# Attention weights times values as two rounded products on the full array, with the weights split by ScalarE and VectorE

## The chip, the cores and the metric

The kernel runs on one core of one Trainium2 chip. The metric is the device time of one execution in microseconds. The engines are TensorE (PE, whose weight loads the profile lists apart as PEld), VectorE (DVE), ScalarE (ACT), GpSimd (POOL) and SyncE (SP, which issues the DMAs).

## What is computed

One inference step of a one-layer trunk on 1024 prompt tokens and 8 running streams of 16 new tokens: three token mixers side by side (stick-breaking attention, Mamba-2, forgetting attention "FoX"), then cross-attention into 256 memory tokens, then a SwiGLU feed-forward, all in float32. The change touches the two attention mixers for the prompt, four heads of 64 columns each:

```
def sb_attend(q, k, v, q_pos, k_pos):
    z = einsum('bqhd,bkhd->bhqk', q, k) * (HEAD_DIM ** -0.5)
    valid = k_pos[None, :] < q_pos[:, None]
    log_keep = where(valid, log_sigmoid(-z), 0.0)
    after = cumsum(log_keep, axis=3, reverse=True) - log_keep
    w = where(valid, exp(log_sigmoid(z) + after), 0.0)
    return einsum('bhqk,bkhd->bqhd', w, v)

def fox_attend(q, k, v, fq, fk, q_pos, k_pos):
    s = einsum('bqhd,bkhd->bhqk', q, k) * (HEAD_DIM ** -0.5) + (fq - fk)
    p = softmax(where(k_pos[None, :] <= q_pos[:, None], s, -inf))
    return einsum('bhqk,bkhd->bqhd', p, v)
```

The last line of each, weights times values, is the product that changes.

## The kernel before

Almost every large product of the kernel is made of three products of rounded numbers: each float32 operand is split into a high part (the value rounded to the short type `fp32r`) and a low part (the rest, rounded too), and `mm3` (L327 to L330) adds high x high, high x low and low x high in PSUM. Such a product goes through PE as one record per instruction.

The prompt's weights times values are not done so. For one head and one pair of 128-query blocks (`qp` = 0 to 3, so 256 queries), `prompt_av` (L571) walks over the key blocks in pairs `kp`. `weights_T` (L575) transposes the weights of two key blocks and two query blocks on PE (L580, into a PSUM bank of the pool `pst`, three banks), and ACT copies the bank to SBUF in float32 (L583, a tile of the pool `pt`, four tiles). The products (L595) take the values `vt` of 128 keys, 64 columns, as the stationary operand and the copied weights as the moving one, both plain float32. For `qp` over 0 the results of even and odd key blocks go to PSUM partitions 0 to 63 and 64 to 127, that is, to the two column halves of PE's array, and four products of two `kp` are issued together, alternating between the halves, so that the two halves can work side by side. For `qp` 0 both go to the first half. At the end ACT copies the upper half and DVE adds the lower (L603, L604; for `qp` 0 one copy, L606), and a DMA writes the 64 x 256 result.

Before that, `load_stacks` (L501) loads for each of the eight heads (four of each mixer) the stacked queries and keys (six DMAs, L507 and L508) and the values (one DMA, L510), from scratch memory in DRAM. `sb_rows` (L513) and `fox_rows` (L528) compute the weights: products on PE (L562 to L565), sigmoids or exponentials on ACT (L519, L520, L542), a scan or a reduction on DVE (L522, L536), and for the first mixer a multiplication on POOL (L132).

The order of the work is set by the scheduler of the tile framework, which places every instruction by its own estimate of time, with hints: `together` (L332) asks that its instructions stand one behind the other, and `hp("av")` (L359) gives `prompt_av` a higher priority. The attention units run woven with other work: the projections of the input (L328 to L330, evacuated at L452 to L456 and L488), the same two attentions of the running streams (L874, L889, L934), the convolution (L772) and the Mamba-2 steps (L1070 to L1162). Each engine then runs its own list strictly in the order given.

Of the kernel before, what the change touches and what calls it, by code (L numbers as in the profile page):

```python
# [8 lines left out]
F32 = mybir.dt.float32  # L9
# [3 lines left out]
ALU = mybir.AluOpType  # L13
# [4 lines left out]
P = 128  # L18
D = 1024
KT = D // P  # L20
SEQ = 1024
# [36 lines left out]
def f32(x):  # L58
    return x.bitcast(F32)
# [3 lines left out]
def tile_hybrid_step(ctx: ExitStack, tc: tile.TileContext, a: dict):  # L63
# [28 lines left out]
    def st_t(dt=F32R):  # L92
        return stp.tile([P, 1024], dt, tag="st", name="st")
# [10 lines left out]
    def pt_t(dt=F32R):  # L104
        return ptp.tile([P, 512], dt, tag="pt", name="pt")
# [129 lines left out]
    v_sc = [dram([T, 256], F32, f"vsc{i}") for i in range(2)]  # L235
# [96 lines left out]
    def together(emits):  # L332

        with tc.high_priority(GROUP):
            first = emits[0]()
            with tc.issue_after(first.ins):
                for f in emits[1:]:
                    f()
# [162 lines left out]
    def load_stacks(m, h):  # L501

        nb, r0 = h // 2, (h % 2) * 64
        iq, ik = 4 * m + nb, 4 * m + 2 + nb
        qs, kh, kl = st_t(), st_t(), st_t()
        for t, i, x0, x1 in ((qs, iq, 0, 1), (kh, ik, 0, 0), (kl, ik, 1, 1)):
            SP.dma_start(out=f32(t[0:64, :]), in_=f32(qk_sc[i, x0, r0:r0 + 64, 0:SEQ]))  # L507
            SP.dma_start(out=f32(t[64:128, :]), in_=f32(qk_sc[i, x1, r0:r0 + 64, 0:SEQ]))  # L508
        vt = st_t(F32)[:, :512].rearrange("p (k d) -> p k d", d=64)
        SP.dma_start(out=vt, in_=v_sc[m][0:SEQ, h * 64:(h + 1) * 64].rearrange("(k p) d -> p k d", p=P))  # L510
        return qs, kh, kl, vt

    def sb_rows(n, pieces):  # L513

# [56 lines left out]
    def prompt_av(h, qp, w0, w1, vt, kt_row):  # L571

        nk = 2 * qp + 2
        po = pO()
        def weights_T(kp):  # L575
            tp = pT()
            o = 0
            for j in range(2):
                for w in (w0, w1) if 2 * kp + j < nk - 1 else (w1,):
                    PE.transpose(tp[:, o:o + P], w[:, (2 * kp + j) * P:(2 * kp + j + 1) * P], ident)  # L580
                    o += P
            pf = pt_t(F32)
            ACT.copy(pf[:, :o], tp[:, :o])  # L583
            return pf

        for k0 in range(0, nk // 2, 2):
            n = min(2, nk // 2 - k0)
            pfs = [weights_T(k0 + i) for i in range(n)]

            def one(i, j, start):  # L590
                last = k0 + i == nk // 2 - 1
                q_, sl = (slice(P, 256), slice(256, 384)) if last and j else (slice(0, 256), slice(j * 256, j * 256 + 256))

                r = 64 * j if qp else 0
                return PE.matmul(po[r:r + 64, q_], vt[:, 2 * (k0 + i) + j, :], pfs[i][:, sl],  # L595
                                 start=start and k0 == 0 and (j == 0 or qp > 0),
                                 stop=k0 + n == nk // 2 and (i, j) in ((0, 0), (n - 1, 1))[qp == 0:])

            order = [(1, 0, True), (0, 1, True), (0, 0, False), (1, 1, False)] if n == 2 else [(0, 0, True), (0, 1, True)]
            together([lambda o=o: one(*o) for o in order])  # L600
        o = sg2_t()[0:64, :256]
        if qp:
            ACT.copy(o, po[64:128, 0:256])  # L603
            DVE.tensor_tensor(out=o, in0=po[0:64, 0:256], in1=o, op=ALU.add)  # L604
        else:
            ACT.copy(o, po[0:64, 0:256])  # L606
        r0 = (h % 2) * 64
        SP.dma_start(out=mix_sc[kt_row, r0:r0 + 64, qp * 256:(qp + 1) * 256], in_=o)

# [1455 lines left out]
```

## Time and profile before

| | |
|---|---|
| median of 3 runs | 1897.55 us (1896.7 to 1902.05) |
| the profiled execution | 1900.41 us, its span 1897.6 us |
| mean granted TensorE clock of the span | 0.988 |
| DMA | 296.64 MB, mean 156 GB/s |

The span is the time from the first to the last instruction of the profiled execution, and the rest of its 1900.41 us lies around it. All times in a view count from the start of the span. In a group's row, "busy" is the sum of its durations and "mean" that of one; matmuls overlap one another in the pipeline, so what a product costs in a row of products is read from the distance of their starts or ends and not from the duration of one. "Idle before" is the time in which the engine did nothing ahead of an instruction, with the work that ended it; "issue" stands where the profile shows nothing that it waited for.

### The profile page before, as it was taken

The numbers are of one execution on the slowest core, as the hardware profiler recorded it, in microseconds if no ns is written. First come the engines' busy times: TensorE is split into PE (matmuls) and PEld (weight loads), VectorE is DVE, ScalarE is ACT, GpSimd is POOL, SyncE is SP. The second block draws the span as 40 slices with busy tenths as digits, with TensorE's granted clock in tenths as the row PEclk, the third lists the DMA queues.
The fourth block names the chain that finished last, engine by engine and source line by source line (L and its number), as shares of the span: only waits on it lengthen the run. The fifth ranks groups of instructions, "written<-read, shape, count | busy, mean of one in ns | idle before, by whom it ended". The sixth has DMA issues, their size and how long they took to land.

```text
span 1897.6 us, 32376 instructions
## 1 busy us (share of the span) xinstructions
PE 1832.7 (97%) x12120; PEld 1637.1 (86%) x12120; DVE 890.6 (47%) x1802; ACT 822.0 (43%) x1751; POOL 618.0 (33%) x923
## 2 busy tenths in 40 slices
PE   7999989999988899999999989999999999999998
PEld 5899878888966767899988879999999999788886
DVE  3412332566556863444444586333333333355554
ACT  6533543545567662344332474333333333344443
POOL 7622434535116652111112107445444542000000
PEclk9999999999999999999999999999999999999999
DMA  9464753537768773345576124333222233656572
GB/s 339 143 189 148 219 153 111 167 94 211 223 199 277 242 254 114 111 134 173 173 278 210 64 76 110 81 87 77 70 70 70 70 79 100 210 181 236 180 241 89
DMA packets 291069, 296.64 MB, mean 156 GB/s; under 512 B 80092, under 2 KB 242884, under 8 KB 290912
## 3 DMA queue, kind: packets, MB, share of 16 engines
q1 hardware_dynamic: 290912, 294.57, 49.6%
q8 instruction: 95, 1.56, 0.3%
q14 instruction: 62, 0.51, 0.1%
HBM read 225.12 MB, written 69.91 MB: 155 GB/s over the span
## 4 chain that ended last, share of the span: by engine, by line
PE 81%; DMA 7%; DVE 4%; POOL 4%; issue 2%; ACT 2%; SPq 1%; POOLq 0%; DVEq 0%; ACTq 0%
PE psd L1867 11%; PE psd L328 9%; PE psd L329 9%; PE psd L330 9%; PE pst L1867 8%; PE pss L1867 4%; PE pss L328 3%; PE pss L329 3%; PE pss L330 3%; POOL wl L132 2%; PE pso L1867 2%; PE pst L328 2%; PE pst L329 1%; PE pso L595 1%; PE pst L330 1%
## 5 line engine op out<-in xcount | busy, mean ns | idle before, releaser
L132 POOL TENSOR_TENSOR wl<-wr,wh 128x256 fp32r<-128x256 f32 (+2 forms) x184 | 138.8, 788 | 232.7 <-ACT wh L292 228.1
L330 PE MATMUL psd<-act,wl 128*128 128x384 f32 x528 | 180.8, 343 | 0.7 <-POOL wl L132 0.7
L328 PE MATMUL psd<-act,wh 128*128 128x384 f32 x528 | 181.4, 344 | 0.0
L329 PE MATMUL psd<-act,wh 128*128 128x384 f32 x528 | 180.7, 342 | 0.0
L1867 PE MATMUL pst<-bT,tr 128*128 128x256 f32 (+1 forms) x1068 | 155.0, 293 | 0.0
L1867 PEld LDWEIGHTS pst<-bT,tr 128*128 128x128 f32 x1068 | 144.9, 188 | 0.1
L330 PE MATMUL psd<-wh,act 128*128 128x512 f32 (+3 forms) x424 | 136.1, 322 | 0.0
L329 PE MATMUL psd<-wl,act 128*128 128x256 f32 (+3 forms) x414 | 133.5, 323 | 1.1 <-POOL wl L132 1.1
L328 PE MATMUL psd<-wh,act 128*128 128x256 f32 (+3 forms) x414 | 132.7, 324 | 1.2 <-DMA act<-osc 1.1
L1867 PE MATMUL psd<-bT,tr 128*128 128x320 f32 (+1 forms) x912 | 132.8, 295 | 0.6 <-POOL tr L132 0.6
L1867 PEld LDWEIGHTS psd<-bT,tr 128*128 128x128 f32 x912 | 124.8, 188 | 1.0 <-POOL tr L132 0.9
L132 POOL TENSOR_TENSOR tr<-u,tr 128x256 fp32r<-128x256 f32 x110 | 82.5, 779 | 101.2 <-ACT tr L1703 83.3
L253 POOL TENSOR_SCALAR sm<-sm 128x1 f32<-128x1 f32 (+2 forms) x27 | 7.1, 261 | 299.9 <-ACT y L1969 211.7
L1842 DVE TENSOR_TENSOR tr<-tr,pst 128x256 f32<-128x256 f32 (+1 forms) x86 | 38.6, 449 | 139.7 <-ACT tr L1839 106.4
L330 PEld LDWEIGHTS psd<-act,wl 128*128 128x128 f32 x528 | 99.2, 188 | 3.4 <-issue 1.9
L132 POOL TENSOR_TENSOR ws<-ws 128x256 f32<-128x256 f32 (+2 forms) x100 | 69.8, 725 | 98.3 <-DVE ws L522 85.2
L328 PEld LDWEIGHTS psd<-act,wh 128*128 128x128 f32 x528 | 99.4, 188 | 2.1 <-issue 1.6
L329 PEld LDWEIGHTS psd<-act,wh 128*128 128x128 f32 x528 | 99.3, 188 | 1.9 <-issue 1.5
L132 POOL TENSOR_TENSOR tr<-raw,tr 128x256 fp32r<-128x256 f32 x94 | 69.2, 766 | 83.6 <-ACT tr L1703 75.3
L1703 ACT CAST tr<-tr 128x384 fp32r<-128x384 f32 (+1 forms) x70 | 37.7, 538 | 117.3 <-DMA tr<-hidsc 114.0
L292 ACT CAST wh<-wr 128x512 fp32r<-128x512 f32 (+2 forms) x90 | 52.3, 621 | 81.3 <-PE psd L330 31.9
L328 PEld LDWEIGHTS psd<-wh,act 128*128 128x128 f32 x414 | 78.8, 191 | 9.9 <-issue 2.0
(637 smaller groups left out, 4763.5 us busy)
## 6 DMA issues: line engine op xcount, KB each, us to landing
u<-w_down SPq DMA_DIRECT2D x40, 512.0 KB
raw<-w_down SPq DMA_DIRECT2D x26, 512.0 KB
st<-qksc SPq DMA_DIRECT2D x48, 256.0 KB
wr<-w_in SPq DMA_DIRECT2D x44, 256.0 KB
tr<-hidsc SPq DMA_DIRECT2D x57, 192.0 KB
hidsc<-tr SPq DMA_DIRECT2D x34, 288.0 KB
qksc<-sg SPq DMA_DIRECT2D x48, 192.0 KB
wr<-cache_sb_k SPq DMA_DIRECT2D x32, 256.0 KB
```

The lines of the kernel that those rows point to most:

```text
L132: POOL.tensor_tensor(out=out[:, a0:a1], in0=in0[:, a0:a1], in1=in1[:, a0:a1], op=op)
L253: POOL.tensor_scalar(v, ss, inv, EPS, ALU.mult, ALU.add)
L292: ACT.copy(hi, raw)
L328: PE.matmul(out, ah, bh, start=start, stop=False)
L329: PE.matmul(out, ah, bl, start=False, stop=False)
L330: PE.matmul(out, al, bh, start=False, stop=stop)
L595: return PE.matmul(po[r:r + 64, q_], vt[:, 2 * (k0 + i) + j, :], pfs[i][:, sl], start=start and k0 == 0 and (j == 0 or qp > 0), stop=k0 + ...
L1703: ACT.copy(hi, src)
L1842: DVE.tensor_tensor(out=at(out, g), in0=at(x, g), in1=ps[g][:, :GW[g]], op=op)
L1867: PE.matmul(dst[g][:, :GW[g]], x[:, ka], y[:, k, :], start=start and k == 0 and m == 0, stop=stop and k == 3 and m == 2, skip_group_check= ...
```

## The change

The values of a head get both parts: the DMA puts them into the low half of a tile of 128 columns per key block, ACT writes their rounding into the high half, DVE overwrites the low half with the difference (L512, L513 of the changed kernel). The transposed weights are split the same way by `split` (L449): ACT writes the rounding (L452), DVE the difference (L453), into two tiles. For each key block there are two products instead of one: low weights and high weights, each with the 128 columns of high and low values as the stationary operand, all added in one PSUM region of 128 partitions; the copy and addition at the end (now for `qp` 0 too) bring the two halves together. A group of four such products is issued per `kp`.

```
-        vt = st_t(F32)[:, :512].rearrange("p (k d) -> p k d", d=64)
-        SP.dma_start(out=vt, in_=v_sc[m][0:SEQ, h * 64:(h + 1) * 64].rearrange("(k p) d -> p k d", p=P))
-        return qs, kh, kl, vt
+        vt = st_t().rearrange("p (k x d) -> p k x d", x=2, d=64)
+        vh, vl = vt[:, :, 0], vt[:, :, 1]
+        SP.dma_start(out=f32(vl), in_=v_sc[m][0:SEQ, h * 64:(h + 1) * 64].rearrange("(k p) d -> p k d", p=P))
+        ACT.copy(vh, f32(vl))
+        DVE.tensor_tensor(out=vl, in0=f32(vl), in1=f32(vh), op=ALU.subtract)
+        return qs, kh, kl, vt.rearrange("p k x d -> p k (x d)")
...
-            pf = pt_t(F32)
-            ACT.copy(pf[:, :o], tp[:, :o])
-            return pf
-
-        for k0 in range(0, nk // 2, 2):
-            n = min(2, nk // 2 - k0)
-            pfs = [weights_T(k0 + i) for i in range(n)]
-
-            def one(i, j, start):
-                last = k0 + i == nk // 2 - 1
+            ph, pl = pt_t(), pt_t()
+            split(ph[:, :o], pl[:, :o], tp[:, :o])
+            return pl, ph
+
+        for kp in range(nk // 2):
+            last = kp == nk // 2 - 1
+            w = weights_T(kp)
+
+            def one(j, x):
                 q_, sl = (slice(P, 256), slice(256, 384)) if last and j else (slice(0, 256), slice(j * 256, j * 256 + 256))
-
-                r = 64 * j if qp else 0
-                return PE.matmul(po[r:r + 64, q_], vt[:, 2 * (k0 + i) + j, :], pfs[i][:, sl],
-                                 start=start and k0 == 0 and (j == 0 or qp > 0),
-                                 stop=k0 + n == nk // 2 and (i, j) in ((0, 0), (n - 1, 1))[qp == 0:])
-
-            order = [(1, 0, True), (0, 1, True), (0, 0, False), (1, 1, False)] if n == 2 else [(0, 0, True), (0, 1, True)]
-            together([lambda o=o: one(*o) for o in order])
+                return PE.matmul(po[:, q_], vt[:, 2 * kp + j, :], w[x][:, sl],
+                                 start=kp == 0 and (j, x) == (0, 0), stop=last and (j, x) == (1, 1))
+
+            together([lambda o=(j, x): one(*o) for j in range(2) for x in range(2)])
         o = sg2_t()[0:64, :256]
-        if qp:
-            ACT.copy(o, po[64:128, 0:256])
-            DVE.tensor_tensor(out=o, in0=po[0:64, 0:256], in1=o, op=ALU.add)
-        else:
-            ACT.copy(o, po[0:64, 0:256])
+        ACT.copy(o, po[64:128, 0:256])
+        DVE.tensor_tensor(out=o, in0=po[0:64, 0:256], in1=o, op=ALU.add)
```

In all, 160 float32 products become 320 rounded ones (256 of 256 columns, 64 of 128), 80 copies become 80 rounding copies and 80 subtractions, and eight copies, eight subtractions and eight additions come new. The scheduler places everything anew, but only up to the output projection: the last 7126 instructions of PE's list (from within that projection on), 1004 of DVE's, 875 of ACT's, 432 of POOL's and 441 of SP's stand in the same order as before.

On PE, the products of the first head's second query pair, before. Rows give the line, the operation, its destination and sources (`pso` is the PSUM region of the result, `pt` the copied weights, `st` the values, `act` and `wh`, `wl` the projection, `wr` a key cache) and the size.

```order
L328 MATMUL psd<-act,wh 128x384
L329 MATMUL psd<-act,wh 128x384
L330 MATMUL psd<-act,wl 128x384
L889 MATMUL pst<-ident,wr 128x128 x2
L595 MATMUL pso<-pt,st 64x256 x3
L595 MATMUL pso<-pt,st 64x128
L889 MATMUL pst<-ident,wr 128x128 x6
L328 MATMUL psd<-act,wh 128x384
```

The same place in the changed kernel, where L884 is the line that was L889:

```order
L329 MATMUL psd<-act,wh 128x384
L595 MATMUL pso<-pt,st 128x256 x4
L884 MATMUL pst<-ident,wr 128x128 x4
L330 MATMUL psd<-act,wl 128x384
L328 MATMUL psd<-act,wh 128x384
L329 MATMUL psd<-act,wh 128x384
L330 MATMUL psd<-act,wl 128x384
L595 MATMUL pso<-pt,st 128x256 x2
L595 MATMUL pso<-pt,st 128x128 x2
L884 MATMUL pst<-ident,wr 128x128 x8
```

One group of four products of 64 columns has become two groups of four products of 128 columns, each behind its own `kp`, with projection products between them.

On DVE, a step of Mamba-2 beside the third FoX head, before (`act` is the state, `sg` the output, `sm` small sums of a norm, `psd` and `pss` PSUM banks):

```order
L1086 TENSOR_TENSOR act<-act 128x512 x2
L1097 TENSOR_TENSOR sg<-psd,act 128x512
L1103 TENSOR_TENSOR act<-act,psd 128x512
L255 SCALAR_TENSOR_TENSOR sm<-sm 128x1
L256 TENSOR_TENSOR sm<-sm 128x1
L257 SCALAR_TENSOR_TENSOR sm<-sm 128x1
L536 ISA ws,sm<-pss,ws 128x512
```

The same step in the changed kernel (each line from the attention on is five less, or three more inside `fox_rows`):

```order
L1081 TENSOR_TENSOR act<-act 128x512 x2
L1092 TENSOR_TENSOR sg<-psd,act 128x512
L453 TENSOR_TENSOR pt<-pst,pt 128x384
L1098 TENSOR_TENSOR act<-act,psd 128x512
L255 SCALAR_TENSOR_TENSOR sm<-sm 128x1
L453 TENSOR_TENSOR pt<-pst,pt 128x512
L256 TENSOR_TENSOR sm<-sm 128x1
L257 SCALAR_TENSOR_TENSOR sm<-sm 128x1
L539 ISA ws,sm<-pss,ws 128x512
```

Two of the new subtractions stand inside the step, one ahead of the update of the state and one inside the chain of the norm.

On ACT, the copy of the first head's high values in the changed kernel (`so` is a result of the value projection, `wh` a weight's high part, `sg` a query or key):

```order
L488 COPY so<-psd 128x256
L292 CAST wh<-wr 128x512 x2
L512 CAST st<-st 128x8x64
L455 ACTIVATE sg<-psd 128x384
L452 CAST pt<-pst 128x384
L522 ACTIVATE ws<-pss 128x384
L523 ACTIVATE ws<-pss 128x384
```

The copy (L512) is new; it waits for the DMA of the values, and what follows it in the list comes behind it.

## The prediction

> **What bounds the kernel now.** I read the page first: the share of each engine, the slices, and the chain of work that ended last.
>
> ```profile
> span 1897.6 us, 32376 instructions
> PE 1832.7 (97%) x12120; PEld 1637.1 (86%) x12120; DVE 890.6 (47%) x1802; ACT 822.0 (43%) x1751; POOL 618.0 (33%) x923
> PE   7999989999988899999999989999999999999998
> DVE  3412332566556863444444586333333333355554
> PE 81%; DMA 7%; DVE 4%; POOL 4%; issue 2%; ACT 2%; SPq 1%; POOLq 0%; DVEq 0%; ACTq 0%
> ```
>
> TensorE (PE) is covered for 97% of the span and holds 81% of the chain, VectorE (DVE) 4%. So an edit that takes work off PE is worth its size wherever PE is full, and work added to DVE and ScalarE (ACT) is worth its size only where PE waits for them.
>
> The changed lines run between 155 and 705 us. Busy times of that stretch in two parts, first of all instructions, then of L595 (weights times values) alone:
>
> ```profile
> 155.00:500.00 345.00, 332.42 (x2447) 295.13 (x2446) 164.99 (x294) 165.34 (x376) 134.42 (x207) 0.99 0.54 158
> 500.00:705.00 205.00, 188.22 (x1524) 147.04 (x1523) 134.25 (x387) 136.30 (x298) 100.58 (x168) 0.96 0.79 250
> ...
> 155.00:500.00 345.00, 24.20 (x164) 10.88 (x164) 0.99 0.54 158
> 500.00:705.00 205.00, 23.36 (x156) 10.23 (x156) 0.96 0.79 250
> ```
>
> The columns are PE, PE weight loads, DVE, ACT, POOL, then granted clock, DMA share and GB/s. Part one is PE's: 332 of 345 us covered, DVE under half busy. In part two DVE rises to 134 of 205 us (65%) and the DMA share to 0.79. The chain, by line, in the same two parts:
>
> ```profile
> by line: PE psd L328 16.4%; PE psd L329 16.4%; PE psd L330 16.1%; POOL wl L132 5.2%; PE pso L595 4.8%; PE pst L580 4.0%; PE pst L889 3.8%; issue 3.3%; POOL ws L132 2.9%; DMA qksc<-sg 2.6%; DMA wr<-w_in 2.5%; DVE xc L772 2.1%; PE pss L562 1.
> by line: DMA wr<-cache_fox_k 10.2%; DMA act<-acsc 8.5%; PE pst L580 5.9%; PE pso L595 5.5%; issue 3.7%; DMA s_ssm<-act 3.5%; PE psd L1133 3.3%; PE pst L889 3.3%; PE psd L328 3.2%; POOL act L1031 3.2%; PE psd L1155 3.1%; PE psd L330 3.0%; PE
> ```
>
> L595 is on the chain for 4.8% of 345 us (16.6 us) and 5.5% of 205 us (11.3 us). In part two the two largest entries are loads.
>
> **The change on PE.** First what a group of today's products costs. L595 does each 64-column float32 product as two records (320 records for 160 products), two products at a time in the two column halves of the array. Timeline of PE at two groups, and PE's weight loads at a third:
>
> ```profile
> 190.03 0.38 PE L889 MATMUL pst<-ident,wr 128*128 128x128 f32 x2
> 190.34 1.08 PE L595 MATMUL pso<-pt,st 128*64 128x256 f32 x8
> 191.35 0.88 PE L889 MATMUL pst<-ident,wr 128*128 128x128 f32 x6
> ...
> 690.47 0.47 PE L328 MATMUL pss<-wh,ws 128*128 128x512 f32 x1
> 690.88 0.65 PE L595 MATMUL pso<-pt,st 128*64 128x256 f32 x4
> 691.46 0.66 PE L580 MATMUL pst<-ident,ws 128*128 128x128 f32 x4
> ...
> 699.99 0.63 PEld L595 LDWEIGHTS pso<-pt,st 128*64 128x64 f32 x8 [0.36 <-issue]
> 700.99 0.14 PEld L925 LDWEIGHTS pst<-ident,ws 128*128 128x128 f32 x1 [0.38 <-issue]
> ...
> 160.76 0.79 PE pso L595 x4
> ...
> 426.14 1.78 PE pst L889 x16
> ```
>
> A group of eight records ends 1.01 us after the work before it (190.41 to 191.42). The six transposes after it end 0.81 us later; sixteen in a row took 1.78, so six need 0.66, and 0.15 is lost on leaving. Weight loads stand still 0.36 us on entering and 0.38 on leaving, with nothing to wait for ("issue"): the array empties when it goes from 128 columns to 64 and back. Eight records cost 1.16 us. Four records on two halves end 0.59 after their predecessor, with 0.15: 0.74. Four records of the first block pair, on one half alone (the chain's 0.79): 0.94. A head has four groups of eight, one of each other kind; eight heads make 32 x 1.16 + 8 x 0.74 + 8 x 0.94 = 50.5 us.
>
> Afterwards there are 320 full-width one-pass products, 256 of 256 columns and 64 of 128. The nearest rows are cross-attention's, which has the same form already:
>
> ```profile
> 853.54 0.28 PE L328 MATMUL pso<-pt,vt 128*128 128x256 f32 x1
> 853.66 0.28 PE L329 MATMUL pso<-pt,vt 128*128 128x256 f32 x1
> 853.78 0.28 PE L330 MATMUL pso<-pt,vt 128*128 128x256 f32 x1
> 853.90 0.38 PE L1522 MATMUL pst<-ident,pt 128*128 128x128 f32 x2
> ```
>
> A start every 0.12 us (0.118 where it runs longer, by my estimate). For 128 columns no row stands alone; half of that, 0.06, and the whole are the ends, and I take 0.07, near the half. 256 x 0.118 + 64 x 0.07 = 34.7 us. No change of array shape is left, so nothing is lost on entering or leaving. Off PE: 50.5 - 34.7 = 15.8 us, by counts of records (164 and 156) 8.1 in part one and 7.7 in part two.
>
> The Trainium skill, "TensorE: Matmul & The Clock Gate", section LDWEIGHTS, gives a load its columns over 1.2 GHz, 107 ns for 128: if the 64 short products are each held to their load, they take 6.8 us and the gain is 13.5. No run here shows it.
>
> A rule that speaks against the change is the skill's "TensorEngine Tiling (Array Packing)", section When to Use Tiling: at 64 columns or fewer, column tiles give up to twice the rate. The rows agree that two tiles run together (four records in 0.59 on two halves, 0.79 on one), but here each holds a two-record float32 product, and the other half of the width will hold the low values; by the rule alone the new products would take 2 x 34.7 us and the kernel would be about 19 us slower.
>
> How much of 15.8 reaches the end? The chain holds 16.6 us of L595 in part one, where its groups without the leaving loss make 43.3 x 164/320 = 22.2, so 75%; where the chain leaves PE there, PE is covered all the same (332 of 345), so between 75 and 100%; I take 90%: 7.3 us. In part two it is 11.3 of 21.1, 53%: 4.1 us. Together 11.4.
>
> **The change off PE.** Each of the 80 copies of transposed weights (L583) becomes a rounding copy by ACT, of the same size, and a subtraction by DVE. The prices, and who waited for L583:
>
> ```profile
> L1157 DVE TENSOR_TENSOR sg<-sg,psd 128x512 f32<-128x512 f32 x9 | 6.1, 682 | 10.3 <-PE psd L1155 10.3
> L453 DVE TENSOR_TENSOR sg<-psd,sg x9: 557/557/558, 98.4 to 221.9; 128x384 fp32r<-128x384 f32 x9
> L1707 DVE TENSOR_TENSOR tr<-u,tr 128x512 fp32r<-128x512 f32 x64 | 42.6, 689 | 6.7 <-ACT tr L1703 4.0 <-PE psd L329 0.7 <-PE pss L1867 0.7
> L604 DVE TENSOR_TENSOR so<-pso,so 64x256 f32<-64x256 f32 x24 | 9.8, 410 | 6.8 <-ACT so L603 6.7
> L292 ACT CAST wh<-wr 128x512 fp32r<-128x512 f32 x82 | 47.4, 620 | 77.4 <-PE psd L330 31.9 <-DMA wr<-w_in 9.2 <-issue 9.1
> ...
>   PEld pso L595: 0.4, 2
>   PE pso L595: 0.2, 1
> ```
>
> DVE gets 48 x 0.682 + 32 x 0.557 = 50.6 us of subtractions, 8 x 0.689 = 5.5 for the low values, and 8 x 0.41 = 3.3 where the first pair of blocks now also adds two halves: 59.4 us, some 30 in each part. ACT gets 8 x 0.62 = 5.0. Products waited 0.6 us in all for their weights, so the subtraction's own 0.7 us is mostly hidden by the matmuls placed between transposes and products; without that cover, 80 x 0.7 = 56 us would be the price. What isn't hidden is the queue: DVE works in order, and behind a subtraction that waits for ACT stand the scans and the state updates for which PE waits, and the bank of transposes is held longer by the same 0.7. The lower end is 0 (DVE stands idle 180 and 71 us). For the value I let a microsecond more on DVE cost what share DVE has in the chain: 4% in part one (the page's figure), a tenth in part two, where rows like these stand on it:
>
> ```profile
> 608.80 1.57 DVE act L1080 x3
> ...
> 645.44 1.72 DVE act L1080 x5
> ```
>
> 30 x 0.04 + 29 x 0.1 = 4.1 us; that tenth is an estimate. The eight copies of the high values now put the load of v into ACT's queue: behind each stand the evacuations (L455, L519, L520) that free PE's banks. Bounds are 0 and about 1.5 us each (the 1.48 us for which SP issued one such load on the chain, below); I take 0.05 each, near zero, since each stands behind other copies: 0.4. It issues no more DMAs than before.
>
> ```profile
> 216.63 1.48 SPq L510
> ```
>
> Sum: 11.4 - 4.1 - 0.4 = 6.9 us off. The profiled execution took 1900.41 us, 2.8 around its span of 1897.6; the median of the runs is 1897.55, so against it 6.9 us give 1890.6, and I say 1890.5.
>
> **The rivals.** A: PE is the bound throughout and DVE's work is hidden: 15.8 - 0.8 = 15 off, 1882.5. For it: 97% cover, 332 of 345. Against: the loads in part two's chain. B: the gain is swallowed. Part two ends by its loads, so PE reaches them earlier and waits longer; then only 7.3 - 4.5 = 2.8 remain, 1894.8. For it speak 18.7% of part two's chain on two loads; against it, that L595 and L580 hold 11.4% there.
>
> C, the slower side: DVE becomes the bound in part two. Its in-order waits there include
>
> ```profile
> DVE sg L1157 <- PE psd L1155: 10.3, 4, 6.0
> DVE act L1080 <- DMA act<-acsc: 6.8, 4, 3.3
> ```
>
> and 134 busy plus 29 added leave 42 of 205 us. It decides once such waits exceed that 42 us, so that subtractions stand ahead of state updates for which PE is idle. With half of the 29 us on the path and part two's PE gain unused: -7.3 + 14.5 = 7.2 slower, 1904.7. Against it: the scheduler placed the subtractions between other DVE work, and PE itself is covered for 188 of the 205 us.
>
> D: the change doesn't do what it says, and the new products still take two records each on the full width. The chain's 0.79, less the 0.36 that ends with the first record, leaves 0.43 for one record of 256 columns and two of 128, so 0.217 for 256 and half of it for 128: 512 x 0.217 + 128 x 0.109 = 125 us against 50.5, about 1972. The cross-attention rows, on tiles of the same types, speak against it. The tiling rule of the skill, taken alone, ends on the same side, near 1917, and shares this chance.
>
> **How the numbers follow.** Forecast 0.48, A 0.22, B 0.16, C 0.12, D 0.02. A measurement here can tell about 0.3% from no change, 5.7 us, so faster means under 1891.9. The forecast lies close to that line: of its 0.48 I give 0.36 to the faster side and 0.12 to no change. Faster 0.36 + 0.22 = 0.58; the same 0.12 + 0.16 = 0.28; slower 0.14. The range is 1880 to 1902: it holds the forecast, B, and A at 1882.5, and leaves out D, most of C and an A in which leaving a group costs more than 0.15 us (together about 0.16).
>
> **What would show it.** Right: L595 at 320 full-width records with starts 0.12 us apart and no 0.36 us of "issue" before them; the span from 155 us to the end of the last such product shorter by 5 to 9 us, most of it before 500; everything after 705 us as before, shifted. DVE 59 us busier. Wrong on price: new PE waits on the subtraction (pt, L453) or on its scans, of more than 5 us; ACT idle for the load of v. Wrong on mechanism: new products spaced 0.2 us or more, or PE idle in part two up by as much as its work fell. A time under 1880 or over 1902 would say that a term is missing.

## The result, and the profile after

| | before | after |
|---|---|---|
| median, us | 1899.16 (1896.7 to 1902.05, 4 runs) | 1923.03 (1914.92 to 1924.65, 4 runs) |
| profiled execution, us (its span) | 1900.41 (1897.6) | 1923.11 (1921.4) |
| mean granted clock of that span | 0.988 | 0.984 |

The ratio after to before is 1.0098, 95% interval 1.0073 to 1.0124: slower by 19 us by the ratio and by 23 to 24 between the profiled executions and between the medians, where 7 us faster was forecast and 1902 was the upper end. (Before has one more run here than when the prediction was made.) The page of the changed kernel, first the span and the engines' shares, then the chain that ended last:

```profile
span 1921.4 us, 32544 instructions
...
PE 1832.3 (95%) x12120; PEld 1663.3 (87%) x12120; DVE 942.9 (49%) x1898; ACT 828.8 (43%) x1759; POOL 621.0 (32%) x923
...
PE 75%; DMA 9%; DVE 6%; issue 3%; POOL 3%; ACT 3%; SPq 1%; DVEq 0%; POOLq 0%; ACTq 0%
```

PE is busy as long as before (1832.3 against 1832.7 us), though its products became cheaper, and the span is 23.8 us longer. PE's share of the chain fell from 81 to 75%, DVE's rose from 4 to 6%, loads' from 7 to 9%. Where the time went is told by two windows: the stretch with the changed lines (which now ends at 730 us, not 705), and all behind it. The columns are length, then PE, PE weight loads, DVE, ACT, POOL, then clock, DMA share, GB/s. Of before, the first:

```profile
155.00:705.00 550.00, 520.64 (x3969) 442.17 (x3968) 299.25 (x680) 301.64 (x674) 235.00 (x375) 0.98 0.63 192
```

Of after, both, and the two parts that the prediction spoke of:

```profile
155.00:730.00 575.00, 520.75 (x3978) 466.89 (x3976) 351.66 (x776) 309.87 (x684) 239.68 (x378) 0.97 0.61 184
730.00:1921.40 1191.40, 1169.28 (x7313) 1067.20 (x7312) 543.42 (x1016) 445.41 (x946) 300.31 (x421) 0.99 0.42 132
...
155.00:500.00 345.00, 319.18 (x2321) 295.93 (x2320) 180.53 (x310) 158.95 (x360) 138.31 (x208) 0.96 0.50 149
500.00:705.00 205.00, 180.06 (x1469) 153.20 (x1471) 157.20 (x437) 138.17 (x302) 94.34 (x159) 0.99 0.77 238
```

The last window is 1191.4 us long, where before had 1192.6: nothing was lost there. The stretch itself grew from 550 to 575 us, and PE is covered for the same 520.7 us of it: all 25 us are new idle time of PE (54.3 us against 29.4). Both parts have it: part one had 12.6 us (345 less 332.42) and now has 25.8.

The changed products. In the first view, of before, and the second, of after, the lines down to "issue" are what PE and its weight loads waited for ahead of them (total us, times), and the lines behind it are who waited for these products:

```profile
L595 PE MATMUL pso<-pt,st x320: 272/379/689, 160.7 to 700.7; 128*64 128x256 f32 x128, 128*64 128x128 f32 x32
...
  issue: 6.3, 28
...
  ACT pt L583: 8.6, 7
```

```profile
L595 PEld LDWEIGHTS pso<-pt,st x320: 186/188/338, 161.6 to 725.3; 128*128 128x128 f32 x160
L595 PE MATMUL pso<-pt,st x320: 220/279/681, 161.8 to 725.3; 128*128 128x256 f32 x128, 128*128 128x128 f32 x32
...
  DVE pt L453: 19.3, 25
...
  issue: 1.0, 2
...
  ACT pt L452: 19.9, 13
  ACT so L600: 12.2, 8
  DVE pt L453: 9.3, 6
```

They are full-width records now, and the "issue" before them, which the prediction put down to the change between 64 and 128 columns, is nearly gone (6.3 us, 28 times before; 1.0 now). In its place stand two waits. Products and their weight loads wait for the subtraction (L453), where they had waited 0.6 us for ACT's copy. The 19.3 us and 25 times of the row add the two engines, so that a group which holds up both counts twice; PE's own part is 8.2 us in 12 places, below. And the other way round, ACT's copy stands for products for 19.9 us, up from 8.6, and DVE's subtraction for 9.3. A copy has no product among its inputs, so what it waits for is its tile: the pool `pt` has four, a pair of key blocks now takes two of them, and a tile comes free only when its products have run. The waits of the stretch by engine (releaser, total us, times, longest) show the second road to PE:

```profile
PE pso L595 <- DVE pt L453: 8.2, 12, 2.4
...
PE pst L884 <- DVE pt L453: 4.4, 2, 2.6
```

L884 transposes the running streams' keys and has nothing to do with the change. It waits for L453 because both use the same three PSUM banks (`pst`), and a bank is now given back by DVE and no longer by ACT. The timeline at one such place:

```profile
250.67 0.52 PE L583 MATMUL pst<-ident,ws 128*128 128x128 f32 x3
...
251.51 1.76 DVE L525 TENSOR_TENSOR_SCAN ws<-ws 128x768 f32<-128x768 f32 x1 [3.02 <-ACT ws L522]
251.61 0.51 ACT L452 CAST pt<-pst 128x384 fp32r<-128x384 f32 x1
...
253.18 0.53 DVE L453 TENSOR_TENSOR pt<-pst,pt 128x384 fp32r<-128x384 f32 x1
...
253.77 0.66 PE L884 MATMUL pst<-ident,wr 128*128 128x128 f32 x4 [2.58 <-DVE pt L453]
```

The transposes end at 251.19. ACT has rounded them by 252.12, and in the old form the bank would have been free then. Now DVE must read it too, and on DVE's list a scan of 1.76 us stands ahead of the subtraction. PE stood for 2.58 us. And a place where ACT stands for a tile:

```profile
243.04 0.49 PE L583 MATMUL pst<-ident,ws 128*128 128x128 f32 x3
...
246.86 0.64 PE L595 MATMUL pso<-pt,st 128*128 128x256 f32 x4
...
247.33 0.28 PE L329 MATMUL psd<-wl,act 128*128 128x260 f32 x1
...
247.41 0.48 ACT L452 CAST pt<-pst 128x384 fp32r<-128x384 f32 x1 [3.71 <-PE pso L595]
...
247.93 0.56 DVE L453 TENSOR_TENSOR pt<-pst,pt 128x384 fp32r<-128x384 f32 x1 [3.49 <-ACT pt L452]
```

These transposes end at 243.53, but ACT can copy them only at 247.41, once the products of an earlier pair have started to end; the bank is held until 248.49, and for 3.71 us nothing else on ACT's list can run. PE did not stop here: it had products of the projection to do. What such a stand of ACT costs PE later can't be read from one place, and the runs with more and fewer tiles have to show it. The same rows give the price of a group of four new products that waits for nothing: 246.86 to 247.33, 0.47 us, 0.118 each. That is the price that the prediction used.

### The profile page after: what moved, and what is told of

Read it like the earlier page. It is cut to its first block, busy times and chain, and to the rows that moved or that the text cites. A ratio compares the mean times of both kernels' runs of the same rounds, so it can differ in the third digit from the quotient of the medians.

```text
span 1921.4 us, 32544 instructions
## 1 busy us (share of the span) xinstructions
PE 1832.3 (95%) x12120; PEld 1663.3 (87%) x12120; DVE 942.9 (49%) x1898; ACT 828.8 (43%) x1759; POOL 621.0 (32%) x923
## 4 chain that ended last, share of the span: by engine, by line
PE 75%; DMA 9%; DVE 6%; issue 3%; POOL 3%; ACT 3%; SPq 1%; DVEq 0%; POOLq 0%; ACTq 0%
PE psd L1862 11%; PE psd L328 9%; PE psd L329 9%; PE psd L330 9%; PE pst L1862 8%; PE pss L1862 4%; PE pss L328 3%; PE pss L330 3%; PE pss L329 3%; DMA act<-acsc 2%; PE pso L1862 2%; POOL wl L132 2%; PE pst L328 1%; PE pst L329 1%; PE pst L330 1%
## 5 line engine op out<-in xcount | busy, mean ns | idle before, releaser
L328 PEld LDWEIGHTS psd<-wh,act 128*128 128x128 f32 x414 | 80.9, 196 | 10.9 <-ACT wh L292 1.9
L330 PEld LDWEIGHTS psd<-wh,act 128*128 128x128 f32 x424 | 82.5, 195 | 6.6 <-issue 1.0
```

Of the source, the lines that this page charges most:

```text
L328: PE.matmul(out, ah, bh, start=start, stop=False)
L330: PE.matmul(out, al, bh, start=False, stop=stop)
```

## The experiments

Five theories stood against one another: that products wait for low weights which come late from DVE (W); that DVE's list is too full, so that other work stands behind the subtractions (Q); that issuing the products pair by pair, each behind its own copy, costs by itself (O); that the values' own split costs (V); and that the second tile of each pair costs (T). A difference of two runs has an interval of some 0.25% (5 us), so single steps of 5 us are at the edge of what can be told apart. Each kernel is also placed anew by the scheduler, and no run tells how much of such a step is the luck of one order. Microseconds behind a ratio are that ratio's distance from 1, times 1900.

**The rounded weights alone.** No subtraction of weights, one tile per pair:

```
-            ph, pl = pt_t(), pt_t()
-            split(ph[:, :o], pl[:, :o], tp[:, :o])
-            return pl, ph
+            ph = pt_t()
+            ACT.copy(ph[:, :o], tp[:, :o])
+            return ph, ph
```

> The changed kernel without the 80 subtractions: both products of a block take the rounded weights, so the low part of the weights is left out and the high part counted twice. PE has the same products. Theory W (products wait for the low weights, which DVE delivers late) and theory Q (59 us more on DVE delay everything that is queued there) both expect the loss gone and most of the gain on PE: 1882 to 1892 us. Theory O (the scheduler's new order of the attention is worse by itself) expects it to stay over 1905. Theory V (the copies of the values stand in ACT's queue and block it) expects 1912 or more.

0.9968, interval 0.9944 to 0.9991: 6 us faster than before. All the loss, and 6 us more, thus hangs on the second tile and the subtraction that fills it. But by the prediction's count 15.8 us were spared on PE, and only 6 arrive, which in part stays open to the end.

**High products first.** The two products that need only the rounding go ahead of the two that need the subtraction:

```
-                                 start=kp == 0 and (j, x) == (0, 0), stop=last and (j, x) == (1, 1))
-
-            together([lambda o=(j, x): one(*o) for j in range(2) for x in range(2)])
+                                 start=kp == 0 and (j, x) == (0, 1), stop=last and (j, x) == (1, 0))
+
+            together([lambda o=(j, x): one(*o) for x in (1, 0) for j in range(2)])
```

> The changed kernel with the two products of the high weights issued ahead of the two of the low ones, so that the subtraction has 0.24 us more. Theory W expects a part of the waits back: some 25 groups by 0.24 us, so 1914 to 1919 against 1923. Theories Q, O and V expect no more than 3 us of difference from the changed kernel.

1.0064, interval 1.0045 to 1.0083. That is 0.34% under the change, little more than the two intervals allow, so something of W seems to be true, but most of the loss stays. PE's waits for the subtraction fell, while ACT and DVE still stood for products:

```profile
DVE pt L453 <- PE pso L595: 16.4, 8, 2.9
...
ACT pt L452 <- PE pso L595: 14.8, 13, 2.2
...
PEld pso L595 <- DVE pt L453: 5.8, 8, 1.8
...
PE pso L595 <- DVE pt L453: 3.1, 4, 1.6
```

**DVE's load alone.** The kernel before, with 80 subtractions of the same sizes, whose results go to an unused half of the values' tile and are read by nobody:

```
-        vt = st_t(F32)[:, :512].rearrange("p (k d) -> p k d", d=64)
+        vfull = st_t(F32)
+        vt = vfull[:, :512].rearrange("p (k d) -> p k d", d=64)
...
-        return qs, kh, kl, vt
+        return qs, kh, kl, (vt, vfull[:, 512:1024])
...
+        vt, dm = vt
...
+            DVE.tensor_tensor(out=dm[:, :o], in0=tp[:, :o], in1=pf[:, :o], op=ALU.subtract)
```

> The kernel before with 80 subtractions of the same shape added on DVE (transposes minus their copy, written to an unused half of a tile that nobody reads). No product waits for them, but the bank of transposes is held until they are done. Theory Q expects 12 to 25 us slower than before, 1910 to 1925. Theory W expects at most 5 us slower, under 1904, since nobody waits for the result. If holding the bank is what costs, it is slower by 5 to 15 with transposes (L580, L889) waiting for DVE.

1.0017, interval 0.9997 to 1.0036: 3 us for some 50 us of DVE work, with no change at all just inside the interval. Q is small here at most, and fits the 4.1 us that the prediction gave it.

**The values.** Two DMAs bring each head's values into both halves of the tile; ACT's copy and DVE's subtraction of them are gone:

```
-        SP.dma_start(out=f32(vl), in_=v_sc[m][0:SEQ, h * 64:(h + 1) * 64].rearrange("(k p) d -> p k d", p=P))
-        ACT.copy(vh, f32(vl))
-        DVE.tensor_tensor(out=vl, in0=f32(vl), in1=f32(vh), op=ALU.subtract)
+        for x in (vl, vh):
+            SP.dma_start(out=f32(x), in_=v_sc[m][0:SEQ, h * 64:(h + 1) * 64].rearrange("(k p) d -> p k d", p=P))
```

> The changed kernel with the values loaded by two DMAs into both halves in place of one DMA, a copy on ACT and a subtraction on DVE; the unrounded values are counted twice. The weights are split as in the change. Theory V expects 8 us or more back, 1915 or less. Theories W and Q expect at most 4 us, since 5.5 of 59 us leave DVE, so 1918 to 1924. Theory O expects a change of either sign with the new order.

1.0105, interval 1.0074 to 1.0136: no gain at all. The 8 us that V asked for are out. A smaller cost could hide in the interval and behind the eight added DMAs.

**Two tiles without a subtraction, and its control.** ACT copies each pair in two halves, once into two tiles and once into one. Nothing is subtracted, and both have the same copies and products. Two tiles:

```
-            ph, pl = pt_t(), pt_t()
-            split(ph[:, :o], pl[:, :o], tp[:, :o])
-            return pl, ph
+            pa, pb = pt_t(), pt_t()
+            ACT.copy(pa[:, :256], tp[:, :256])
+            ACT.copy(pb[:, 256:o], tp[:, 256:o])
+            return pa, pb
...
-                return PE.matmul(po[:, q_], vt[:, 2 * kp + j, :], w[x][:, sl],
+                return PE.matmul(po[:, q_], vt[:, 2 * kp + j, :], w[j][:, sl],
```

The control differs from it in these lines, and its products take `w[x]` again, which is the same tile for both:

```
-            pa, pb = pt_t(), pt_t()
+            pa = pt_t()
...
-            ACT.copy(pb[:, 256:o], tp[:, 256:o])
-            return pa, pb
+            ACT.copy(pa[:, 256:o], tp[:, 256:o])
+            return pa, pa
```

> As the kernel without subtractions, but the rounded weights of a pair of key blocks go into two tiles of the pool pt, one per key block, by two smaller copies on ACT; each product of a block takes the rounded weights twice (the low part is left out). As many of the four pt tiles are taken as in the change, and DVE has no subtraction. Theory T (the change loses by its tiles: a pair now takes two of four, so ACT and DVE stand waiting for the products to free one) expects half of the 25 us or more to come back: 8 us or more slower than before. Theory W (the wait for the low weights) expects the time of the kernel without subtractions, 3 to 8 us under before.

> The kernel without subtractions in which ACT writes the rounded weights by the same two smaller copies as in the kernel with two tiles (1.0087), but into one tile. High weights are counted twice, low ones left out. Theory T expects 0.996 to 1.000, the difference being the second tile. If the 13 us more on ACT cost it, 1.006 or more.

Two tiles: 1.0087, interval 1.0066 to 1.0108. One tile: 0.9973, interval 0.9956 to 0.9990. The second tile by itself makes 1.14%, 22 us, with no work added on any engine. O is out as the cause of the loss, since the control issues its products pair by pair too and is faster than before. In the first kernel ACT's second copy (L587) and its first (L586) stand for products for 22.4 us:

```profile
ACT pt L587 <- PE pso L596: 12.9, 11, 2.7
...
ACT pt L586 <- PE pso L596: 9.5, 10, 2.0
```

With one tile it is 6.0 us:

```profile
ACT pt L586 <- PE pso L596: 6.0, 6, 2.0
```

**The subtraction done, but not read.** The change with its second tile filled as ever, where the products read the rounded weights twice (low weights left out of the result):

```
-            return pl, ph
+            return ph, ph
```

> The changed kernel with its subtractions, bank held and second tile taken, but the products read the high weights twice and nobody reads the low ones. Theory W expects nearly the time of the kernel without subtractions, within 3 us, as no product waits for DVE. Theory Q (the load on DVE) expects 10 us or more above that. Theory T expects little loss, since the second tile is free as soon as it is written.

1.0024, interval 1.0008 to 1.0040. Here a second tile is given back as soon as the subtraction has ended and not only by products; the kernel is 5 us slower than before, where the change is 19 by its ratio. But it is 11 us above the rounded weights alone, which neither W nor T expected and Q did. Its trace shows that the tiles have a part in it all the same. ACT's copy now stands for a tile that the subtraction holds, where it had stood for products:

```profile
ACT pt L452 <- DVE pt L453: 17.8, 13, 3.2
```

A later run, with the subtraction done in another pool, comes to 0.9996.

**The kernel before with a second tile that nobody reads.** As the run on DVE's load, but the results go to a tile of `pt`:

```
+            dm = pt_t(F32)
+            DVE.tensor_tensor(out=dm[:, :o], in0=tp[:, :o], in1=pf[:, :o], op=ALU.subtract)
```

> The kernel before with the 80 added subtractions written into a second pt tile that nobody reads, in place of the unused half of another tile (1.0017). Theory T expects 5 to 15 us more than that, 1.0045 to 1.01, because DVE, in order, now waits for a tile that products hold. Theory Q (only the load on DVE counts) expects the same 1.000 to 1.004.

1.0042, interval 1.0028 to 1.0056, against 1.0017 with the results elsewhere: even for so short a stay, and with the old products, the tile costs about 5 us (0.25%, as large as the uncertainty of the difference).

**A fifth tile.** High products first and five tiles in `pt`; for the room the ring of raw weights (`wr`) goes from four buffers to three. The control has three raw buffers and four tiles:

```
-        return ptp.tile([P, 512], dt, tag="pt", name="pt")
+        return ptp.tile([P, 512], dt, tag="pt", name="pt", bufs=5)
...
-        return ring.tile([P, 528], F32, tag="wr", name="wr", bufs=4)
+        return ring.tile([P, 528], F32, tag="wr", name="wr", bufs=3)
```

> High products first, with five pt tiles in place of four; the room comes from the raw weights of the projections, three tiles in place of four. Theory T expects 5 us or more under the kernel with high products first (ratio 1.0064 to before). Theory W expects within 3 us of it.

> High products first, with three tiles of raw weights in place of four and four pt tiles: the control of the kernel with five pt tiles (1.0132). Theory T expects that taking the raw tile costs much and that the fifth pt tile gave some of it back: 1.015 or more. If the fifth tile gives nothing, 1.011 to 1.015.

1.0132, interval 1.0112 to 1.0152, and for the control 1.0170, interval 1.0150 to 1.0191. Taken alone the first number would have spoken against T; the control shows that the lost raw buffer cost 20 us (1.0170 against 1.0064) and that the fifth tile gave 7 back. What it mended is the waiting for tiles, not PE's for the subtraction, which came to 11.3 and 7.9 us (weight loads and products) against 8.8 and 5.1 in the control. In the control, then with the fifth tile, DVE and ACT stand for products:

```profile
ACT pt L452 <- PE pso L595: 18.6, 11, 5.1
...
DVE pt L453 <- PE pso L595: 17.1, 9, 2.9
```

```profile
DVE pt L453 <- PE pso L595: 6.5, 4, 2.2
ACT pt L452 <- PE pso L595: 6.5, 5, 2.3
```

**The low weights in another pool.** High products first, and the low weights in a tile of the pool `sg`. That pool has four tiles of the same size too, which other steps share (the expectations further down call it the larger pool):

```
-            ph, pl = pt_t(), pt_t()
+            ph, pl = pt_t(), sg_t(F32R)
```

> High products first, and the low weights go into a tile of the pool sg (four tiles of the same size, used by other steps) in place of pt, so that a pair of key blocks takes one pt tile as before the change. All else as in the kernel with high products first (1.0064). Theory T (the loss is the second pt tile: ACT and DVE stand in their queues until products free one) expects a ratio of 0.997 to 1.003 and ACT's waits for the products under 8 us (14.8 there). Theory W (the subtraction is simply late) expects 1.004 or more.

1.0035, interval 1.0018 to 1.0052: 0.29% under the run with high products first, 0.63% under the change. ACT's waits for products at this copy fell from 14.8 to 2.0 us. The kernel is still slower than before; a new wait has come, for a `sg` tile that products hold, on POOL, and PE still waits for the subtraction:

```profile
POOL sg L738 <- PE pso L595: 15.9, 3, 10.2
...
ACT pt L452 <- PE pso L595: 2.0, 1, 2.0
...
PEld pso L595 <- DVE sg L453: 4.5, 12, 1.4
```

**The next pair's transposes first.** `weights_T(kp + 1)` is called ahead of the products of `kp`, in three kernels: the one with high products first, the one with low weights in `sg`, and the one with the rounded weights alone.

```
+        ws = [weights_T(0)]
...
-            w = weights_T(kp)
+            if not last:
+                ws.append(weights_T(kp + 1))
+            w = ws[kp]
```

> High products first, and the transposes of the next pair of key blocks are issued ahead of the products of this one, so that PE has work while DVE subtracts. Theory W expects most of the remaining 9 us of waits for DVE gone and a ratio to before of 0.998 to 1.002. Theory T expects no gain or a loss, because two pairs now hold all four tiles at once.

> The change with the low weights in a tile of the larger pool (as the run at 1.0035), products of high weights first, and the next pair's transposes ahead of this pair's products, so that a pair's subtraction has the time of another pair's transposes and products to end. If what is left after the tiles is PE waiting for the subtraction, 0.998 to 1.001; if it is VectorE's queue itself (scans and state updates behind the subtractions), 1.002 to 1.005.

> The kernel that reads the rounded weights twice (no subtraction, low weights left out), but with the next pair's transposes placed ahead of this pair's products, so that two pairs are under way as in the kernel before; four tiles still hold four pairs. It was 0.9968 without that. If the missing 10 us of PE's gain lie in the order (each pair's products right behind its own copy), 0.990 to 0.994. If the stretch swallows them whatever the order, 0.996 to 0.998.

1.0083 (interval 1.0060 to 1.0107) beside 1.0064; 1.0053 (1.0036 to 1.0069) beside 1.0035; 0.9973 (0.9957 to 0.9989) beside 0.9968. None is faster than its twin. The runs say little on W. In the first pair PE's own wait for the subtraction even rose, from 3.1 to 6.2 us. In the second it came out the same in number and size,

```profile
PEld pso L598 <- DVE sg L453: 4.5, 12, 1.4
```

so the order that the scheduler made had not given the subtraction more time. That the missing gain lies in where each pair's products stand behind their own copy is not borne out either.

**Does this stretch pass PE's gain on at all?** The kernel before, with two products left out of each group of four:

```
-            order = [(1, 0, True), (0, 1, True), (0, 0, False), (1, 1, False)] if n == 2 else [(0, 0, True), (0, 1, True)]
+            order = [(1, 0, True), (0, 1, True)] if n == 2 else [(0, 0, True), (0, 1, True)]
```

The mark of a sum's last product (`stop`) moves with them.

> The kernel before, with two of the four products of each of its 32 groups of four left out (half of the key blocks in those groups don't count). Nothing changes on ScalarE, VectorE or in the tiles; by the rows of before PE is spared 32 x (1.16 - 0.74) = 13.4 us, nearly as much as by the change. If PE time in this stretch reaches the end as the prediction had it (72%), the ratio to before is about 0.995 (9.7 us), and the change's lost 15.8 us must have gone to what its new steps cost. If the stretch swallows PE's gain (rival B: loads, other engines' chains), it is 0.9975 or above, and the kernel without subtractions had no more to win than it did.

0.9938, interval 0.9919 to 0.9957: 11.8 us of the 13.4 that PE was spared, 88% (the interval allows 8 to 15 us). With the old products the stretch passes most of PE's gain on. So what the change lost was mostly spent by the change.

**The subtraction in the other pool, not read.** As the run with low weights in `sg`, but `return ph, ph`:

> As the run with low weights in the larger pool's tiles (1.0035), but the products read the rounded weights twice: the subtraction is done, in its tile, and nobody waits for it (low weights are left out). With no subtraction at all the same products gave 0.9968. If the 0.67% between the two is VectorE's queue (what stands behind the subtractions), this run stays near 1.002 to 1.004; if it is products waiting for low weights, it comes down to 0.997 to 0.999; between, both.

0.9996, interval 0.9983 to 1.0008. Between the rounded weights alone (0.9968) and this run lies DVE's list, and the stay in the `sg` tile: 0.28%, 5 us. Between this run and the one whose products read the low weights (1.0035) lies the waiting: 0.39%, 7 us, in which PE's waits for the subtraction and POOL's for a `sg` tile held by products can't be told apart. In this run products wait for ACT's copy for 1.2 us and for nothing on L453:

```profile
  ACT pt L452: 1.2, 3
```

**The first mixer alone.** The new form, with low weights in `sg` and high products first, for the stick-breaking heads; the old form for the others. The old function stands beside the new one as `prompt_av_1`, the old load of values returns for the second mixer (`m` = 1), and the call chooses:

```
-                    lambda w: prompt_av(h, qp, w[0], w[1], env["st"][3], 2 * m + h // 2))
+                    lambda w: (prompt_av_1 if m else prompt_av)(h, qp, w[0], w[1], env["st"][3], 2 * m + h // 2))
```

> The new form, with its low weights in the larger pool's tiles and products of high weights first, for the four stick-breaking heads alone (the stretch up to about 500 us, which PE bounds); the forgetting heads keep the old form. If the tiles were the fault and PE's gain in the first part arrives: 7.3 us less by the prediction's terms, some of it lost to the subtractions, 0.996 to 0.999. If the first part pays for the subtractions as much as the second does, 1.001 to 1.003.

1.0016, interval 0.9999 to 1.0033: no gain, as the record expected for the case that the first part pays for the subtractions as much as the second does. No version that computes the whole was faster than the kernel before. The run ahead of this one points to the reason: with no second `pt` tile and nobody waiting for low weights, the new form stands at 0.9996.

## Why the prediction was wrong

**The size of PE's work, 15.8 us: nearly right.** A new group of four costs 0.47 us, as 4 x 0.118 said, and the stop on going between 64 and 128 columns is nearly gone. Over whole traces it is a little less. Count each PE record from its start, or from the end of the record before it where that is later, to its own end. By that, L595 took 44.3 us before and 37.5 with the rounded weights alone, and the records behind its groups took some 7.5 and 2.0 us longer than their like elsewhere: about 12.3 us spared. The products of 128 columns, priced at 0.07 us, took 0.09 on average.

**How much of it reaches the end: right for the old products, too high for the new.** The prediction let 11.4 of 15.8 us through, 72%. Products left out of the kernel before came through at 88%, so that rival B, that the stretch swallows the gain, was not the cause of the loss. But the three kernels with the new products and no subtraction of weights gained only 5 to 6 us (0.9968, 0.9973, 0.9973), and the intervals of the last two end at 8. About 5 us of the forecast gain are missing before any subtraction is added.

**The values' copies on ACT, 0.4 us: not contradicted.** Without them nothing was gained, but the run can't tell 0.4 us from several. ACT did stand 5.4 us, in five places, for the loads of the values.

**DVE's fuller list, 4.1 us: it fits.** Measured were 3 us beside the old products and 5 beside the new ones, each with an uncertainty nearly as large. DVE's busy time rose by 52 us (942.9 less 890.6) where 59 were counted; the subtractions of weights themselves took 50.3, as forecast.

**The step that failed** is the one that set the rest of the price to nothing: "the subtraction's own 0.7 us is mostly hidden by the matmuls placed between transposes and products", with the bank of transposes "held longer by the same 0.7". It counted the work of the subtraction and not what is held while it is awaited. Three things were missing. The split doubles the tiles per pair, and `pt` has four: the diff shows `pt_t()` twice where it stood once, the words on the kernel give the number of tiles, and no term took it up. By itself this is worth 22 us (two tiles against one, no subtraction). In the change, where it overlaps with the other waits, what remains is smaller: with high products first, taking the low weights out of `pt` brings 6 us (1.0064 to 1.0035). Second, products wait for low weights: 7 us, in which POOL's wait for a `sg` tile is included. Third, the bank is not held for 0.7 us more but until DVE's list reaches the subtraction, 2.58 us of PE at the place shown; this one is part of the 3 to 5 us of DVE's list. The prediction reckoned that the matmuls in between would hide most of 56 us, but they were not always there when a subtraction came late.

As a sum over the runs, from the rounded weights alone to the change: -6 (0.9968), +5 DVE's list (0.9996), +7 products that read the low weights (1.0035), +6 their tile in `pt` (1.0064), +6 low products first (1.0098). Each step has an uncertainty of some 5 us. The waits share the same time, so that another road gives the same causes other shares: by the run whose subtraction fills a `pt` tile that nobody reads (1.0024) it is -6, +11 and +14. The total, some 25 us, is the same on both.

**The slower rival, C**, had the sign and little of the cause: DVE is not the bound in part two (157 of 205 us busy), and half of PE's new idle time lies in part one, where DVE is busy for 181 of 345 us. That PE waits for what stands in order on DVE's list is true at single places, such as the 2.58 us above.

**What stays open** is why only 6 of the 15.8 us arrived with the rounded weights alone. By the traces about 3.5 were never spared (15.8 against 12.3). Another 5.5 or so is granted clock: the span times the lost share of the clock, averaged over all runs, is 28.4 us for that kernel and 22.9 for the kernel before in the same session. The kernel before with products left out lost only 2.5 us more than the kernel before in its session (24.2 against 21.7). Why the clock was lower wasn't tried by itself. It does not come with the new products alone: with the subtraction in `sg`, read or not, 24.1 and 23.2 us were lost. So the 5 us of DVE's list above would be about 10 if the clock had stayed the same, and the shares in the sum over the runs are mixed with the clock. The change itself lost 30.2 us over its four runs. By the profiled runs it is 1921.4 x 0.016 = 30.7 against 1897.6 x 0.012 = 22.8, so 8 us more. That would be about half of why PE's busy time didn't fall with its work; the other half isn't assigned.

## What to carry to other kernels

When a copy out of PSUM is split into two results, count its tiles and its readers before its work: a pool of four that held four pairs holds two, each engine stands in order at the missing tile, and the bank behind it stays taken until the last reader, in that reader's own list, has come to it. An engine that is half idle can still be a poor place to give a bank back, if its list has long instructions ahead of short ones. And measure the counterpart of a buffer moved (a raw buffer fewer cost 20 us here) before reading a number as evidence on the buffer gained.

## What was not expected of the hardware

One short wait of PE was paid about twice here. Of the changed kernel, PE around the longest wait of a product for a subtraction, and the granted clock (the column behind POOL) in the windows behind it:

```profile
325.30 1.76 DVE L525 TENSOR_TENSOR_SCAN ws<-ws 128x768 f32<-128x768 f32 x1 [2.93 <-ACT ws L522]
...
326.98 0.53 DVE L453 TENSOR_TENSOR pt<-pst,pt 128x384 fp32r<-128x384 f32 x1
...
327.57 0.75 PE L595 MATMUL pso<-pt,st 128*128 128x256 f32 x4 [2.44 <-DVE pt L453]
...
331.73 0.42 PE L329 MATMUL psd<-wl,act 128*128 128x264 f32 x1
...
331.95 0.42 PE L330 MATMUL psd<-wh,act 128*128 128x264 f32 x1
```

```profile
327.50:328.50 1.00, 0.93 (x6) 0.93 (x7) 0.01 (x1) 0.33 (x1) 1.00 (x3) 0.76 0.00 0
328.50:329.50 1.00, 0.68 (x4) 0.28 (x3) 0.82 (x3) 0.95 (x4) 0.47 (x1) 0.50 0.04 8
329.50:331.00 1.50, 1.50 (x8) 1.50 (x8) 1.03 (x6) 0.83 (x3) 0.00 (x0) 0.50 0.92 240
331.00:334.50 3.50, 3.50 (x17) 3.50 (x17) 0.54 (x1) 0.46 (x1) 0.00 (x0) 0.50 0.50 141
334.50:336.00 1.50, 1.50 (x13) 1.50 (x12) 0.00 (x0) 0.24 (x1) 0.00 (x0) 0.88 0.00 0
```

PE had no work for 2.44 us. About half a microsecond after it had work again the clock fell to half, and stayed there for over 6 us, with products 0.22 us apart in place of 0.12. Each window's length times its lost share of the clock gives 0.24 + 0.5 + 0.75 + 1.75 + 0.18 = 3.4 us, an estimate of what was lost besides the wait itself.

The Trainium skill, "TensorE: Matmul & The Clock Gate", Part 1, says that PE drops to half rate after an idle window of about 3.4 us and comes back after as long a busy one. The halving agrees, but here 2.44 us of idling were followed by it, while the 2.58 us at 251 were not (the clock was 1.00 up to 262 us). That the idling brought it on is thus not shown.

```profile
253.00:256.00 3.00, 2.23 (x19) 2.23 (x20) 1.60 (x6) 1.26 (x3) 2.58 (x6) 1.00 0.90 249
...
259.00:262.00 3.00, 3.00 (x27) 3.00 (x27) 0.18 (x2) 0.51 (x2) 0.00 (x0) 1.00 0.35 114
```
